# Router sums pinned later, further blocks spread over the expert loop, and each pair combined in two places

## The chip, the cores and the metric

One core of a Trainium2 chip runs the whole layer. The metric is the device time of one execution in microseconds.

## The reference

One decoder layer on 512 tokens of width 1024, in float32. A token mixer of three branches ends in an output projection; a layer norm follows; then a mixture of experts; then a second layer norm. What matters here, cut:

```python
x = layer_norm(DN_ALPHA * x + mix, ln1_g, ln1_b)
p_grp = softmax(x @ w_grp + b_grp)            # 4 groups, top 1
p_in  = softmax((x @ w_exp + b_exp)[group])   # 8 experts in the group, top 2
h = silu(xb @ w_gate[e]) * (xb @ w_up[e]);  y = h @ w_down[e]
x = layer_norm(DN_ALPHA * x + sum(weight * y), ln2_g, ln2_b)
```

32 experts of 512 hidden columns, gate, up and down of 2 MB each: 201 MB of weights that are read once.

## The kernel before

**Stages.** The token mixer runs until about 515 us. Then comes `out_proj` with the first norm and the router, then `moe`, the loop over 32 experts, then `final`, the second norm.

**The order.** A scheduler orders each engine's instructions by a model of their times. `keep_in_program_order` pins one instruction behind the one traced just before it on its engine. `inorder` does so when `self.steady` is set, which holds from the last token tile of `out_proj` through `moe`; so TensorE's order in the expert loop is the order of the program, and the other engines' order is the scheduler's.

**`out_proj`.** Two halves of 512 output columns, with products of split numbers (`mm3`, three matmuls each): the first half is 96 matmuls into four banks (4 blocks of `k` by 2 by 4 token tiles by 3), the second goes tile by tile, with transposes, `norm1` and the routing of each tile between. `router_consts` is called ahead of the first half. It loads router weights, biases and, as 4-element runs, the first norm's gain and bias `gb` by ScalarE's queue, multiplies them on VectorE (L933, L934), reduces them to `wsum` (L936), sums these over partitions with a matmul against ones (L938), and makes `nsg` and `br` of the result (L940, L941), which `norm1` uses (L1068, L1069).

**Weights.** SyncE's queue alone loads weights, in 192 pieces of 1 MB (`load_piece`, L1439), in the order in which the experts use them, into a ring of 20 slabs; up to eight are under way. A piece waits until its slab's last reader is done, and everything behind it on the queue waits too. One slab, the `G` slab (`spare`), also holds the gathered rows of pair 1 and, in its second half, small routing tables and then the gain and bias that `residual` uses; it joins the ring late, as the 39th piece.

**The expert loop.** Experts go in pairs of 128 gathered rows, 64 each. For expert `e` TensorE does 32 gate matmuls, the turn (transposes) of the hidden rows of expert `e-1`, 32 up matmuls, and after them `flush`, the `down` of expert `e-1`, whose result ScalarE and VectorE split into `yh` and `yl`. In an odd expert the rows of the next pair are transposed before the flush (`gather_turn`, two "s" banks, copied out by ScalarE and VectorE), and then `combine` adds the pair before to the four token tiles: 16 matmuls of one-hot rows `ot` against `y`, in banks "pt" and "s" by turns, and eight additions to `acc` on VectorE. PSUM has three "mm" banks, two "s", two "pt" and one "o".

**Only in the first experts.** `route_further` (after expert 1's flush, VectorE) finds the tokens beyond 64 of an expert; `slots_everywhere` (expert 2, before its flush) spreads the slots with 16 matmuls and two ScalarE copies; `further_slots` makes the tables of the further blocks with 24 small VectorE operations and eight small matmuls that add up in one "pt" bank, four before expert 2's flush and four after it. `residual` (experts 1 and 2, half of the columns each) loads gain and bias by ScalarE's queue, scales them there (L1089) and multiplies and adds them to `acc` on VectorE (L1092, L1093).

**The middle.** Before expert 16, `overflow` runs a loop over the further blocks, with a count read at run time. In these data the count is 0, so the loop is skipped, but every engine has to arrive (L1558) before any goes on. Sixteen pieces beyond that point are issued ahead of it.

Of the kernel before, what the change touches and what calls it, by code (L numbers as in the profile page):

```python
# [43 lines left out]
class Build:  # L44
# [869 lines left out]
    def router_consts(self, p):  # L914

        nc, I = self.nc, self.I
        V = nc.vector.tensor_tensor
        wr = p.tile([128, KD, 36], F32, name="wr")
        for i in range(2):
            ks = slice(i * 4, i * 4 + 4)  # L920
            nc.scalar.dma_start(wr[:, ks, 0:4], dram(I["router_w_grp"], i * 2048, [[16, 128], [4, 4], [1, 4]]))
            nc.scalar.dma_start(wr[:, ks, 4:36], dram(I["router_w_exp"], i * 16384, [[128, 128], [32, 4], [1, 32]]))
        br = p.tile([128, 36], F32, name="br")
        nc.scalar.dma_start(br[:, 0:4], dram(I["router_b_grp"], 0, [[0, 128], [1, 4]]))
        nc.scalar.dma_start(br[:, 4:36], dram(I["router_b_exp"], 0, [[0, 128], [1, 32]]))
        for i, nm in enumerate(("ln1_g", "ln1_b")):
            nc.scalar.dma_start(self.gb[:, i].rearrange("p (i k) -> p i k", i=2), dram(I[nm], 0, [[4, 128], [512, 2], [1, 4]]))
        ones = p.tile([128, KD, 128], F32, name="xT", bufs=2)[:, 0]
        nc.gpsimd.memset(ones, 1.0)
        bc = [128, KD, 36]  # L930
        wb = p.tile([128, KD, 128], F32, name="xT", bufs=2)[:, :, 0:36]
        sm = p.tile([128, 2, 36], F32, name="wsum")
        V(wb, wr, self.gb[:, 1, :, None].to_broadcast(bc), OP.mult)  # L933
        V(wr, wr, self.gb[:, 0, :, None].to_broadcast(bc), OP.mult)  # L934
        for i, t in enumerate((wr, wb)):
            nc.vector.tensor_reduce(sm[:, i], t.rearrange("p k n -> p n k"), axis=AX.X, op=OP.add)  # L936
        ps = self.bank("o")
        nc.tensor.matmul(ps[:, 0:72], ones, sm.rearrange("p i n -> p (i n)"), start=True, stop=True)  # L938
        nsg = p.tile([128, 36], F32, name="nsg")
        nc.vector.tensor_scalar(nsg, ps[:, 0:36], -1.0, None, op0=OP.mult)  # L940
        V(br, br, ps[:, 36:72], OP.add)  # L941
        return wr, nsg, br

    def out_proj(self, mh, ml):

# [4 lines left out]
        for tt in range(NT):  # L950
# [5 lines left out]
        rc = self.router_consts(p)  # L956

        def evac(half, tt, a):
            o = R[tt][:, half * 512:(half + 1) * 512]
# [12 lines left out]
                 for k4 in range(4)]  # L972
        for tt in range(NT):
            evac(0, tt, accs[tt])

        rows = [self.bank("s") for _ in range(2)]
        lg = p.tile([128, NT, 36], F32, name="lg")
# [94 lines left out]
    def norm1_apply(self, p, tt, mv, rs):  # L1072
# [7 lines left out]
            nc.scalar.activation(r[:, c], r[:, c], AF.Identity, bias=nm, scale=rs)  # L1080
        nc.gpsimd.dma_start(self.zd[tt * 128:(tt + 1) * 128], r)

    def residual(self, t, c):

        nc = self.nc
        cs = slice(c * 512, (c + 1) * 512)
        for i, nm in enumerate(("ln1_g", "ln1_b")):
            nc.scalar.dma_start(t[:, i], dram(self.I[nm], c * 512, [[0, 128], [1, 512]]))
        nc.scalar.mul(t, t, ALPHA)  # L1089
        for tt in range(NT):  # L1090
            r = self.acc[tt // 2][:, tt % 2, cs]
            self.tc.keep_in_program_order(nc.vector.tensor_tensor(r, r, t[:, 0], OP.mult))  # L1092
            nc.vector.tensor_tensor(r, r, t[:, 1], OP.add)  # L1093


    def first_max(self, p, v, rev, m, oh, name):
# [212 lines left out]
    def further_slots(self, part):  # L1309

        nc = self.nc
        T = nc.vector.tensor_scalar
        p = self.rt
        if part == 0:
            self.fps = self.bank("pt")[0:64, 0:32]
        for tt in (part * 2, part * 2 + 1):
            for i in range(2):
                rk = self.og0[:, tt % 2 * 2 + i, 0:64]
                wo = p.tile([128, 2, 16], F32, name="rwo", bufs=4)
                io, bk = self.io128[:, 0:16], self.blk[:, tt, i:i + 1]  # L1320
# [3 lines left out]
                self.inorder(nc.tensor.matmul(self.fps, rk, wo.rearrange("p a n -> p (a n)"), start=(tt == 0 and i == 0),  # L1324
                                              stop=(tt == NT - 1 and i == 1)))
        if part:
            T(self.idxo, self.fps[:, 0:16], 4096.0, None, op0=OP.add)
            for h in range(2):
                T(self.wt48[h * 64:(h + 1) * 64, 32:48], self.fps[:, 16:32], 0.5, None, op0=OP.mult)


    def gather(self, xs, idx):
# [75 lines left out]
            self.inorder(self.nc.tensor.matmul(ps, l, yh[:n, ds_], start=start and i == 0, stop=False))  # L1408
            self.inorder(self.nc.tensor.matmul(ps, l, yl[:n, ds_], start=False, stop=(i == len(terms) - 1)))  # L1409

    def combine(self):

        for tt in range(NT):
            for dh in range(2):
                ps = self.bank("s" if tt % 2 else "pt")
                self.combine_tile(ps, self.terms, tt, dh, True)
                a = self.acc[tt // 2][:, tt % 2, dh * 512:(dh + 1) * 512]
                self.nc.vector.tensor_tensor(a, a, ps, OP.add)  # L1418
        self.terms = []

    def ytile(self, last=False):
        t = self.moe_tile().bitcast(F32R) if last else self.slab("Y", "y", F32R)
# [29 lines left out]
    def moe(self):  # L1452
        p = self.ep
        self.worder, self.wt = [], []
        for e in range(E + 1):
            gu = [(e, m, i) for m in (0, 1) for i in (0, 1)] if e < E else []
            dn = [(e - 1, 2, i) for i in (0, 1)] if e else []
            self.worder += dn + gu if e == 2 * LOOP else gu + dn
        spare = self.spare
        xs1, gb = spare[:, :D], spare[:, D:].rearrange("p (i n) -> p i n", i=2)  # L1460
        xq = self.xq0
        xs = self.xq0.rearrange("p k n -> p (k n)")
        self.db = p.tile([128, 2, S], I16, name="db")
        pairs = E // 2
        pend = None
        self.terms = []

        def fetch(j, xs=xs):
            if j < pairs:
                self.gather(xs, self.idx[:, j:j + 1])  # L1470

        for e in range(E):
            pr, odd = e // 2, e % 2
            if pr == LOOP and not odd:
                self.flush(pend, self.turn(pend[1]))
                self.combine()
                pend = None

                held = self.worder.index((e, 0, 0)) + len(self.ring) - 7
                self.load_until(held)  # L1480
                self.overflow()
                self.npiece = held
                xq = self.gather_turn(xs)
                fetch(pr + 1)
            hT = []
            gu = self.gate_up(xq[:, :, odd * 64:(odd + 1) * 64], self.pieces(e, 0), self.pieces(e, 1),
                              (lambda: hT.append(self.turn(pend[1]))) if pend and e > 1 else None)
            if e == 0:
                self.load_until(len(self.first))
                fetch(1, xs1)  # L1490
                self.slot_weights()
                pend = (0, self.hidden(gu, self.wt48[:, 0:1]), None)
                continue
            if e == 1:
                fetch(2)
                hT.append(self.turn(pend[1]))
            if e == 2:
                self.slots_everywhere()
                self.further_slots(0)
# [260 lines left out]
```

## Time and profile before

| | us |
|---|---|
| median of three executions | 1097.99 |
| their range | 1094.75 to 1098.54 |
| the profiled execution | 1097.79 |
| its span | 1096.1 |
| TensorE, VectorE, ScalarE, GpSimd busy | 999.9, 593.6, 317.0, 201.1 |

The span is the stretch that the profile shows; 1.7 us of the time lie around it. Times in the rows are microseconds from the span's start. PE is TensorE's matmuls, PEld its weight loads, DVE VectorE, ACT ScalarE, POOL GpSimd, SP SyncE; a `q` behind the name is the engine's queue issuing something. A matmul's busy time overlaps the next one's, so TensorE's pace is read from the distance of starts.

### The profile page before, as it was taken

What the parts mean: (1) busy time and instruction counts of PE and PEld (TensorE: products, weight loads), DVE (VectorE), ACT (ScalarE), POOL (GpSimd) and SP (SyncE); (2) the same over time, 40 slices, a digit from 0 to 9 for tenths busy, and PEclk for the clock granted to TensorE, in tenths of its full rate; (3) what the DMA queues carried; (4) which work ended last, traced back from release to release, by engine and by line L of the source; (5) the groups of instructions that cost most, each with busy time, mean ns of one, the idle gap of its engine ahead of it and who ended that gap; (6) DMA issues with size and microseconds to landing.
All of it is one profiled execution on the core that took longest, in us unless ns stands there. A gap on an engine that the chain in (4) does not pass through costs nothing. (4 is left out here: it accounts for less than half of the span.)

```text
span 1096.1 us, 15867 instructions
## 1 busy us (share of the span) xinstructions
PE 999.9 (91%) x6189; PEld 698.7 (64%) x6189; DVE 593.6 (54%) x1427; ACT 317.0 (29%) x662; POOL 201.1 (18%) x179
## 2 busy tenths in 40 slices
PE   7969988999989999999698879999996999999994
PEld 6956676778778777888585455555552655555552
DVE  7992667474788784253255384444444244444436
ACT  4322222334556564232122121111110111111112
POOL 5410213334111223453112000000000000000003
PEclk9995999999999899999899989999998899999997
DMA  6701442225111112735415999999998999999992
GB/s 201 225 1 23 98 82 77 78 71 165 38 39 40 39 39 66 281 115 198 158 74 215 409 382 418 418 418 419 418 419 360 403 418 418 418 418 418 419 375 77
DMA packets 79821, 256.21 MB, mean 234 GB/s; under 512 B 16544, under 2 KB 43712, under 8 KB 55168
## 3 DMA queue, kind: packets, MB, share of 16 engines
q1 hardware_dynamic: 68064, 245.56, 57.4%
q10 hardware_dynamic: 8944, 3.59, 2.1%
q0 software_dynamic: 2736, 6.03, 1.5%
q8 instruction: 49, 0.80, 0.3%
q14 instruction: 28, 0.23, 0.1%
HBM read 254.40 MB, written 4.69 MB: 236 GB/s over the span
## 5 line engine op out<-in xcount | busy, mean ns | idle before, releaser
L1355 PE MATMUL ps_mm<-w,xq 128*64 128x256 f32 x1296 | 148.3, 381 | 0.0
L102 POOL TENSOR_TENSOR whl<-w,whl 128x1024 fp32r<-128x1024 f32 (+3 forms) x41 | 94.7, 2318 | 278.7 <-ACT whl L113 237.9
L1355 PEld LDWEIGHTS ps_mm<-w,xq 128*64 128x64 f32 x1296 | 91.2, 137 | 53.3 <-issue 8.6
L72 PE MATMUL ps_mm<-xh,whl 128*128 128x512 f32 x288 | 115.8, 402 | 0.0
L71 PE MATMUL ps_mm<-xl,whl 128*128 128x512 f32 x288 | 115.4, 401 | 0.0
L70 PE MATMUL ps_mm<-xh,whl 128*128 128x512 f32 x288 | 115.2, 400 | 0.0
L1365 DVE SCALAR_TENSOR_TENSOR th<-th,ps_mm 128x256 f32<-128x256 f32 x32 | 13.5, 421 | 161.2 <-ACT th L1364 161.2
L1393 DVE TENSOR_TENSOR y<-ps_o,y 64x512 fp32r<-64x512 f32 x60 | 41.3, 689 | 86.7 <-ACT y L1391 79.3
L1335 POOL DMA_INDIRECT xq<-zd,idx x14 | 14.0, 1003 | 389.8 <-PE ps_pt L1408 306.3
L1391 ACT CAST y<-ps_o 64x512 fp32r<-64x512 f32 x60 | 34.8, 579 | 141.7 <-issue 81.9
L1387 PE MATMUL ps_o<-w,hT 128*64 128x512 f32 x288 | 69.6, 608 | 0.0
L72 PEld LDWEIGHTS ps_mm<-xh,whl 128*128 128x128 f32 x288 | 54.7, 190 | 11.0 <-issue 0.8
L71 PEld LDWEIGHTS ps_mm<-xl,whl 128*128 128x128 f32 x288 | 54.8, 190 | 10.3
L70 PEld LDWEIGHTS ps_mm<-xh,whl 128*128 128x128 f32 x288 | 54.6, 189 | 10.4 <-issue 0.9
L113 ACT CAST whl<-w 128x1024 fp32r<-128x1024 f32 (+3 forms) x56 | 54.7, 989 | 13.5 <-PE ps_mm L72 13.4
L1355 PE MATMUL ps_mm<-rc,xq 128*64 128x256 f32 x384 | 46.8, 393 | 0.0
L1387 PEld LDWEIGHTS ps_o<-w,hT 128*64 128x64 f32 x288 | 21.4, 139 | 36.0 <-issue 33.0
L1364 ACT ACTIVATE th<-ps_mm 128x256 f32<-128x256 f32 x32 | 12.3, 383 | 104.8 <-PE ps_mm L1355 104.8
L1355 PE MATMUL ps_mm<-rd,xq 128*64 128x256 f32 x368 | 42.2, 381 | 0.0
L1355 PEld LDWEIGHTS ps_mm<-rc,xq 128*64 128x64 f32 x384 | 27.9, 142 | 17.6 <-issue 4.9
L1418 DVE TENSOR_TENSOR acc<-acc,ps_pt 128x512 f32<-128x512 f32 x60 | 38.4, 677 | 0.0
L1418 DVE TENSOR_TENSOR acc<-acc,ps_s 128x512 f32<-128x512 f32 x60 | 38.2, 677 | 0.0
(581 smaller groups left out, 2064.4 us busy)
## 6 DMA issues: line engine op xcount, KB each, us to landing
w<-in_moe_w_up_dram SPq DMA_DIRECT2D x43, 1024.0 KB, 19.9
w<-in_moe_w_gate_dram SPq DMA_DIRECT2D x38, 1024.0 KB, 20.3
w<-in_moe_w_down_dram SPq DMA_DIRECT2D x37, 1024.0 KB, 20.0
w<-in_w_in_dram SPq DMA_DIRECT2D x17, 1024.0 KB, 5.0
rc<-in_moe_w_down_dram SPq DMA_DIRECT2D x14, 1024.0 KB, 19.9
rc<-in_moe_w_gate_dram SPq DMA_DIRECT2D x14, 1024.0 KB, 19.9
rd<-in_moe_w_down_dram SPq DMA_DIRECT2D x13, 1024.0 KB, 20.5
rd<-in_moe_w_gate_dram SPq DMA_DIRECT2D x12, 1024.0 KB, 14.6
```

Of the source, the lines that this page charges most:

```text
L70: mm(ps, a[0], b[0], start=start, stop=False)
L71: mm(ps, a[0], b[1], start=False, stop=False)
L72: mm(ps, a[1], b[0], start=False, stop=stop)
L102: (V if eng == "dve" else P)(dst, src, h, OP.subtract)
L113: pin(self.nc.scalar.copy(hv[:, :, c:c + w], src))
L1335: self.nc.gpsimd.indirect_dma_start(xs[:n], None, self.zd[:, :], bass.IndirectOffsetOnAxis(ap=idx, axis=0), bounds_check=S - 1, oob_is_err ...
L1355: self.inorder(nc.tensor.matmul(gu[hh * 64:(hh + 1) * 64, part * 256:(part + 1) * 256], xe[:, k], w[k // 4][:, k % 4, hh * 256:(hh + 1) * ...
L1365: nc.vector.scalar_tensor_tensor(th, th, 1.0, gu[:, 0:256], op0=OP.add, op1=OP.mult)
L1387: self.inorder(nc.tensor.matmul(y[dh][dh * 64:(dh + 1) * 64], hT[:, q, hh * 64:(hh + 1) * 64], wd[f // 2][:, f % 2, dh * 512:(dh + 1) * 51 ...
L1391: nc.scalar.copy(part(yh, dh), y[dh][dh * 64:(dh + 1) * 64])
L1393: nc.vector.tensor_sub(part(yl, dh), y[dh][dh * 64:(dh + 1) * 64], part(yh, dh).bitcast(F32))
L1418: self.nc.vector.tensor_tensor(a, a, ps, OP.add)
```

## The change

Four parts.

- The sums' matmul with `nsg` and `br` becomes a function that `out_proj` calls after the first half's evacuation; the matmul is pinned there. The loads and products ahead of it stay.
- `residual` loses its loads and its scaling: `gains` issues the loads by GpSimd's queue, the first half at expert 0, the second at expert 1 after the first residual, and the factor goes into VectorE's operations. At expert 1 the residual now stands ahead of `route_further`.
- `slots_everywhere` and the first `slot_rows` move behind expert 2's flush; the two calls of `further_slots` move to experts 4 and 6, each summing in a bank of its own, with a small tile `rfs` between them.
- `combine` takes token tiles and bank tags: tiles 0 and 1 between gate and up of the odd expert, on "s" and "mm", tiles 2 and 3 where all four stood, on "pt" and "mm".

```diff
@@ router_consts, out_proj @@
-        ps = self.bank("o")
-        nc.tensor.matmul(ps[:, 0:72], ones, sm.rearrange("p i n -> p (i n)"), start=True, stop=True)
+        def sums():
+            ps = self.bank("o")
+            self.tc.keep_in_program_order(nc.tensor.matmul(ps[:, 0:72], ones, sm.rearrange("p i n -> p (i n)"), start=True, stop=True))
+            nc.vector.tensor_scalar(nsg, ps[:, 0:36], -1.0, None, op0=OP.mult)
+            V(br, br, ps[:, 36:72], OP.add)
...
             evac(0, tt, accs[tt])
+        sums()
@@ residual @@
+    def gains(self, t, c):
+        for i, nm in enumerate(("ln1_g", "ln1_b")):
+            nc.gpsimd.dma_start(t[:, i], dram(self.I[nm], c * 512, [[0, 128], [1, 512]]))
...
-            nc.scalar.dma_start(t[:, i], dram(self.I[nm], c * 512, [[0, 128], [1, 512]]))
-        nc.scalar.mul(t, t, ALPHA)
...
-            self.tc.keep_in_program_order(nc.vector.tensor_tensor(r, r, t[:, 0], OP.mult))
-            nc.vector.tensor_tensor(r, r, t[:, 1], OP.add)
+            self.tc.keep_in_program_order(nc.vector.scalar_tensor_tensor(r, r, ALPHA, t[:, 0], op0=OP.mult, op1=OP.mult))
+            nc.vector.scalar_tensor_tensor(r, t[:, 1], ALPHA, r, op0=OP.mult, op1=OP.add)
@@ further_slots @@
-            self.fps = self.bank("pt")[0:64, 0:32]
+            self.fsum = p.tile([64, 32], F32, name="rfs")
+        fps = self.bank("pt")[0:64, 0:32]
...
+            nc.vector.tensor_tensor(self.fsum, self.fsum, fps, OP.add)
...
+        else:
+            nc.vector.tensor_copy(self.fsum, fps)
@@ combine @@
-    def combine(self):
-        for tt in range(NT):
+    def combine(self, tiles=range(NT), tags=("pt", "s")):
+        for tt in tiles:
...
-                ps = self.bank("s" if tt % 2 else "pt")
+                ps = self.bank(tags[tt % 2])
@@ moe @@
+            def between():
+                hT.append(self.turn(pend[1]))
+                if self.terms:
+                    self.combine((0, 1), ("s", "mm"))
...
+                self.gains(gb, 0)
...
-            if e == 2:
-                self.slots_everywhere()
-                self.further_slots(0)
-                pend = (*pend[:2], self.slot_rows(self.sid[:, 0:1]))
+            if e in (4, 6):
+                self.further_slots(e // 2 - 2)
...
-                    self.combine()
+                    self.combine((2, 3), ("pt", "mm"))
...
-            if e == 1:
-                srt = self.route_further()
             if e == 2:
-                self.further_slots(1)
-                srt.close()
+                self.slots_everywhere()
+                self.terms[0] = (self.slot_rows(self.sid[:, 0:1]), *self.terms[0][1:])
             if e in (1, 2):
                 self.residual(gb, e - 1)
+            if e == 1:
+                self.gains(gb, 1)
+                srt = self.route_further()
```

## Rows read from the trace of the kernel before

**Rows 1.** The page: busy tenths of the DMA engines in 40 equal slices.
```profile
DMA  6701442225111112735415999999998999999992
```

**Rows 2.** Windows: stretch, length, busy of PE PEld DVE ACT POOL, PEclk, DMA, GB/s.
```profile
690.10:717.90 27.80, 27.14 (x190) 15.67 (x188) 11.67 (x22) 5.33 (x12) 1.00 (x1) 1.00 1.02 420
```

**Rows 3.** Chain of waits that ended last: start, length, what; the last expert.
```profile
1054.51 3.60 PE ps_mm L1355 x32
...
1063.30 3.58 PE ps_o L1387 x16
...
1070.74 0.57 PE ps_o L1387
```

**Rows 4.** Timeline of SyncE's queue; then DMA issues at 1044 to 1049, with landing.
```profile
1045.96 0.33 SPq L1439 DMA_DIRECT2D w<-in_moe_w_down_dram  x1
...
w<-in_moe_w_down_dram SPq DMA_DIRECT2D x1, 1024.0 KB, 20.0
```

**Rows 5.** Timeline, `out_proj`, first half: start, length, engine, line, operation, [idle before <-releaser].
```profile
515.10 0.39 PE L70 MATMUL ps_mm<-whl,mh 128*128 128x512 f32 x1
...
524.62 0.39 PE L70 MATMUL ps_s<-whl,mh 128*128 128x512 f32 x1
...
531.14 0.46 DVE L933 TENSOR_TENSOR xT<-wr,gb 128x288 f32<-128x288 f32 x1 [7.85 <-DMA rc<-in_moe_w_down_dram]
...
533.56 0.63 DVE L936 TENSOR_REDUCE wsum<-wr 128x36 f32<-128x288 f32 x1
...
534.34 0.67 PE L938 MATMUL ps_o<-wsum,xT 128*128 128x72 f32 x2 [9.34 <-DVE wsum L936]
...
538.19 0.40 PE L70 MATMUL ps_mm<-whl,mh 128*128 128x512 f32 x1
...
548.20 0.39 PE L72 MATMUL ps_s<-whl,ml 128*128 128x512 f32 x1
```

**Rows 6.** Windows of two stretches, and SyncE's queue as expert 0 begins.
```profile
534.80:538.20 3.40, 3.40 (x10) 2.68 (x11) 0.29 (x2) 0.93 (x1) 0.00 (x0) 0.53 0.58 243
...
590.00:597.50 7.50, 5.69 (x54) 3.81 (x56) 3.66 (x16) 2.46 (x9) 1.11 (x1) 1.00 0.01 3
...
597.55 0.33 SPq L1439 DMA_DIRECT2D w<-in_moe_w_up_dram  x1
```

**Rows 7.** Waits at 560 to 662: who <- for whom: total, times, longest.
```profile
ACT w L1089 <- DMA w<-in_ln_b_dram: 26.0, 2, 13.4
...
SPq L1439 <- PE ps_o L1387: 11.5, 1, 11.5
```

**Rows 8.** Windows: expert 2's stop, and the notch in the loads after it.
```profile
631.00:639.30 8.30, 1.77 (x13) 1.23 (x12) 8.27 (x28) 0.96 (x2) 0.00 (x0) 0.86 1.01 419
...
640.00:655.00 15.00, 15.00 (x102) 10.23 (x98) 10.60 (x29) 3.52 (x7) 0.31 (x1) 0.87 0.95 352
```

**Rows 9.** Groups by line, 470 to 700: busy, mean ns of one, idle before.
```profile
L1092 DVE TENSOR_TENSOR acc<-acc,w 128x512 f32<-128x512 f32 x8 | 5.5, 682 | 0.5 <-ACT w L1089 0.5
...
L960 DVE SCALAR_TENSOR_TENSOR acc<-acc,ps_mm 128x512 f32<-128x512 f32 x6 | 4.1, 684 | 15.4 <-PE ps_mm L72 15.4
```

**Rows 10.** Timeline of one pair's combination, and of `y` and the turn after it.
```profile
711.91 0.19 PEld L1408 LDWEIGHTS ps_s<-y,ot 128*128 128x128 f32 x1 [1.09 <-ACT xq L1246]
...
714.91 0.20 PEld L1387 LDWEIGHTS ps_o<-w,hT 128*64 128x64 f32 x4 [0.37 <-issue]
...
803.35 1.39 DVE L1393 TENSOR_TENSOR y<-ps_o,y 64x512 fp32r<-64x512 f32 x2 [2.19 <-ACT y L1391]
...
805.43 0.32 PEld L1374 LDWEIGHTS ps_pt<-ident,th 128*128 128x128 f32 x2 [0.39 <-issue]
```

**Rows 11.** SyncE's queue about the skipped loop, and the window of its end.
```profile
828.47 0.33 SPq L1439 DMA_DIRECT2D rc<-in_moe_w_up_dram  x1
849.00 0.34 SPq L1439 DMA_DIRECT2D w<-in_moe_w_up_dram  x1
...
843.00:850.00 7.00, 0.54 (x3) 0.54 (x4) 1.81 (x5) 0.00 (x0) 0.00 (x0) 0.66 0.41 159
```

More of the change, by code (lines that the diff above doesn't have):

```diff
@@ L936, in router_consts @@
             nc.vector.tensor_reduce(sm[:, i], t.rearrange("p k n -> p n k"), axis=AX.X, op=OP.add)
-        ps = self.bank("o")
-        nc.tensor.matmul(ps[:, 0:72], ones, sm.rearrange("p i n -> p (i n)"), start=True, stop=True)
         nsg = p.tile([128, 36], F32, name="nsg")
-        nc.vector.tensor_scalar(nsg, ps[:, 0:36], -1.0, None, op0=OP.mult)
-        V(br, br, ps[:, 36:72], OP.add)
-        return wr, nsg, br
+        def sums():
[3 more added lines that the diff above has]
+            V(br, br, ps[:, 36:72], OP.add)
+        return (wr, nsg, br), sums
     def out_proj(self, mh, ml):
@@ L955, in out_proj @@
               for j in range(2)] for i in range(2)]
-        rc = self.router_consts(p)
+        rc, sums = self.router_consts(p)
         def evac(half, tt, a):
@@ L1081, in norm1_apply @@
         nc.gpsimd.dma_start(self.zd[tt * 128:(tt + 1) * 128], r)
+    def gains(self, t, c):
+        nc = self.nc
+        for i, nm in enumerate(("ln1_g", "ln1_b")):
+            nc.gpsimd.dma_start(t[:, i], dram(self.I[nm], c * 512, [[0, 128], [1, 512]]))
     def residual(self, t, c):
@@ L1086, in residual @@
         cs = slice(c * 512, (c + 1) * 512)
-        for i, nm in enumerate(("ln1_g", "ln1_b")):
-            nc.scalar.dma_start(t[:, i], dram(self.I[nm], c * 512, [[0, 128], [1, 512]]))
-        nc.scalar.mul(t, t, ALPHA)
         for tt in range(NT):
             r = self.acc[tt // 2][:, tt % 2, cs]
-            self.tc.keep_in_program_order(nc.vector.tensor_tensor(r, r, t[:, 0], OP.mult))
-            nc.vector.tensor_tensor(r, r, t[:, 1], OP.add)
+            self.tc.keep_in_program_order(nc.vector.scalar_tensor_tensor(r, r, ALPHA, t[:, 0], op0=OP.mult, op1=OP.mult))
+            nc.vector.scalar_tensor_tensor(r, t[:, 1], ALPHA, r, op0=OP.mult, op1=OP.add)
     def first_max(self, p, v, rev, m, oh, name):
@@ L1323, in further_slots @@
                 T(wo[:, 1], io, bk, self.wk[:, i, tt:tt + 1], op0=OP.is_equal, op1=OP.mult)
-                self.inorder(nc.tensor.matmul(self.fps, rk, wo.rearrange("p a n -> p (a n)"), start=(tt == 0 and i == 0),
-                                              stop=(tt == NT - 1 and i == 1)))
+                self.inorder(nc.tensor.matmul(fps, rk, wo.rearrange("p a n -> p (a n)"), start=(tt % 2 == 0 and i == 0),
+                                              stop=(tt % 2 == 1 and i == 1)))
         if part:
-            T(self.idxo, self.fps[:, 0:16], 4096.0, None, op0=OP.add)
+            nc.vector.tensor_tensor(self.fsum, self.fsum, fps, OP.add)
+            T(self.idxo, self.fsum[:, 0:16], 4096.0, None, op0=OP.add)
             for h in range(2):
-                T(self.wt48[h * 64:(h + 1) * 64, 32:48], self.fps[:, 16:32], 0.5, None, op0=OP.mult)
+                T(self.wt48[h * 64:(h + 1) * 64, 32:48], self.fsum[:, 16:32], 0.5, None, op0=OP.mult)
+        else:
+            nc.vector.tensor_copy(self.fsum, fps)
     def gather(self, xs, idx):
@@ L1418, in combine @@
                 self.nc.vector.tensor_tensor(a, a, ps, OP.add)
-        self.terms = []
+        if NT - 1 in tiles:
+            self.terms = []
     def ytile(self, last=False):
@@ L1485, in moe @@
             hT = []
+            def between():
+                hT.append(self.turn(pend[1]))
+                if self.terms:
+                    self.combine((0, 1), ("s", "mm"))
             gu = self.gate_up(xq[:, :, odd * 64:(odd + 1) * 64], self.pieces(e, 0), self.pieces(e, 1),
-                              (lambda: hT.append(self.turn(pend[1]))) if pend and e > 1 else None)
+                              between if pend and e > 1 else None)
             if e == 0:
@@ L1496, in moe @@
                 hT.append(self.turn(pend[1]))
-            if e == 2:
-                self.slots_everywhere()
-                self.further_slots(0)
-                pend = (*pend[:2], self.slot_rows(self.sid[:, 0:1]))
+            if e in (4, 6):
+                self.further_slots(e // 2 - 2)
+                if e == 6:
+                    srt.close()
             end = pr == pairs - 1
```

## The prediction, made before the changed kernel was seen

> **What bounds the kernel now.** I read the page's slices first, to see where the DMA engines are full, then the windows over the expert loop, then the chain of waits at the end, and only then the timelines of the two places where the loads are not full.
>
> From about 600 us to 1066 us the DMA engines are full but for two notches [rows 1]. One pair of experts takes 27.8 us there, TensorE never rests for long, and the DMA engines run at 420 GB/s, 1.02 of their time [rows 2]. So both are near their limit, and they have to be told apart. A pair needs 12 pieces of 1,048,576 bytes and a gather of 0.52 MB, 13.1 MB, which at 418 GB/s is 31.3 us (an estimate from these rows; one piece is 2.51 us). TensorE takes 27.8 us a pair and so eats 3.5 us a pair of the stock that was loaded ahead. At the end the stock is nearly gone: the last weight piece is issued at 1045.96 us, takes 20.0 us to land, 1065.96 us, and the last `down` begins at 1070.74 us [rows 3, 4]. The loop is thus held by TensorE, with the loads 4.8 us behind it. If TensorE alone gets faster, those 4.8 us are all there is. For more, the stream of loads must start earlier or lose its notches.
>
> **The router's sums.** In the first half of `out_proj` TensorE starts a matmul each 0.227 us (42 steps from 515.10 to 524.62 us). Then it stands until 534.34 us, because the sums' matmul (L938) sits in the middle of the half and waits for `wsum`. VectorE can't make `wsum` before the small loads of gain and bias land: it waits 7.85 us for them and ends `wsum` at 534.2 us. After that TensorE runs near the 1.2 GHz level (granted 0.53) until 538.19 us [rows 5, 6]. The row names a weight load as what VectorE waited for, but L933 reads only `wr` and `gb`, and those are the loads issued last on ScalarE's queue. 96 matmuls at 0.227 us would put the last start at 515.10 + 95 x 0.227 = 536.6 us; it is 548.2 us. Lost: 11.6 us.
>
> After the change the matmul is pinned behind the last matmul of that half, at about 536.9 us. `wsum` is there since 534.2 us, 2.7 us earlier, so nothing waits. The sums still cost their two matmuls, 0.67 us at the lower clock, about 0.35 us at the higher. Their followers on VectorE (`nsg`, `br`) are two small operations, needed only by the first `norm1` some 20 matmuls later. Gain: 11.6 - 0.4 = **11.2 us**. What is late next in this half is nothing that I find: the parts of the second half need buffers that TensorE frees as it goes, and these come free earlier by the same amount.
>
> From 548 us to expert 0 the work is a chain of compute. The first load that opens the full stream is issued at 597.55 us, when expert 0 has freed a slab; before it, from 590 to 597.5 us, the DMA engines do nothing (0.01) [rows 6]. So TensorE and the stream both start 11.2 us earlier.
>
> **Gains by another queue, further blocks later.** Before, ScalarE issues the loads of gain and bias and then waits for them at the head of its queue, 26.0 us in two waits [rows 7]. Behind it stand the copies that feed `down`. Expert 2 also holds `further_slots`, for which TensorE waits on VectorE: of 8.3 us it works 1.77 [rows 8]. While TensorE stands, slabs don't come free: SyncE's queue waits 11.5 us for a `down` [rows 7], and the DMA engines fall to 352 GB/s over 15 us [rows 8]. That notch is 15 x (418 - 352) / 418 = **2.4 us** of loads.
>
> The change takes the wait from ScalarE. GpSimd issues the four loads; behind them on its queue stand only the gathers, needed half a pair later. VectorE's sixteen operations stay sixteen: a scalar_tensor_tensor of this shape is 684 ns, the multiply 682 ns [rows 9], so folding in the factor costs nothing. The route's operations on VectorE now come behind the first residual (8 x 0.68 = 5.5 us), so `slots_everywhere` may wait for `dd` up to 5.5 us. The second residual may wait for its load up to 13 us, the longest such wait before [rows 7], with VectorE's later work behind it. Both lie on TensorE's side only. The 24 small operations of `further_slots`, two additions on `fsum` and its eight matmuls move to experts 4 and 6, beside matmuls. I take the notch as gone: 2.4 us, bounds 0 and 2.4.
>
> **The combination in two places.** In each odd expert the second group of combining matmuls waits 1.09 us for a bank that the gather's copies still read [rows 10]. The new first half stands between gate and up on one "s" pair and one "mm" pair, where no copy is running; the second half uses "pt" and "mm". Matmuls and additions are as many as before. The new risk is `y`: the additions need the pair's second `down`, whose subtraction ends at 803.35 + 1.39 = 804.7 us, while the half would begin after the turn at 805.43 us plus 0.4 us. That leaves about 1 us, so no wait. Value: about 1.1 us a pair for TensorE, bounds 0 and 1.5, and **nothing** on the clock while the loads hold the pair at 31.3 us.
>
> **The middle.** At the skipped loop of further blocks SyncE issues nothing from 828.5 to 849.0 us, since every engine has to arrive; the eight loads under way run dry, and 843 to 850 us moves 159 GB/s [rows 11], 7 x 259 / 418 = **4.3 us** of loads. TensorE arrives later than the loads by a stock that the change makes smaller: TensorE gains 11.2 us, the stops of expert 1 and 2 and 5 x 1.1 us until there, the loads 13.6 us. By some 13 us it comes earlier against them, and the notch is 4.3 us. I take all of it; bounds 0 and 4.3.
>
> **The sum.** The last piece lands at 1065.96 - 11.2 - 2.4 - 4.3 = 1048.1 us. TensorE has gained at least 11.2 + 6.5 (expert 2's stop) + 13 x 1.1 = 32 us, so it now waits for loads. The last `up` lands four pieces earlier, 1038.1 us; then its 16 matmuls (half of 3.60), half a combination (2.0, as 12 of its matmuls take 3.0), `down` of expert 30 (3.58), the opening matmuls of two tiles and a turn (3.9, from that `down`'s end to the next) and the last `down` (3.6) [rows 3, 10]: 1053.0 us, where it now ends at 1074.3. That is 21.3 us. The profiled execution took 1097.79 us with a span of 1096.1, 0.2 below the median of 1097.99. 1097.8 - 21.3 = **1076.5 us**.
>
> **The rivals.** First, **only the start moves**: the notches stay, because the second residual's load or the barrier stops SyncE's queue as before, or the sums' loads land more than 2.7 us later than here and part of the stop stays (the change then doesn't do what it says in that place). With 11.2 us alone it is 1087 us. For it: both new loads of gain and bias go through full DMA engines. Against it: up to eight loads of 2.51 us are under way, so a stop of the queue must outlast 20 us. Second, **the stream opens earlier still**: SyncE's queue keeps its order, and at 597.55 us one slab's wait holds back four pieces for other memory. If these pass it, up to 8 us of idle DMA time [rows 6] are used: 1068 us. Third, **slower by the clock**: once TensorE waits for each piece, about 0.8 us in 2.5, the granted clock falls to 1.2 GHz, and a pair costs some 53 us in place of 31.3. One such pair eats the gain; with two it is about 1120 us. For it: after the stop at 524.8 us TensorE ran at the lower level for 3.9 us [rows 5, 6]. Against it: from 590 to 597.5 us TensorE worked 5.69 of 7.5 us in short stretches and the granted clock stayed 1.00 [rows 6], and at the lower level TensorE becomes the slower side, works without a stop and gets its clock back.
>
> The Trainium skill speaks for this third case: "TensorE: Matmul & The Clock Gate", section "HAM oscillation — how this bites in real kernels", tells of a loop that waits for a DMA at each weight tile and falls to half clock at every one. By that rule the last pairs would be slower as priced above. The row from 590 to 597.5 us doesn't agree for waits as short as these; no row here has a longer run of them.
>
> **How the numbers follow.** Forecast 0.62, only the start 0.20, earlier stream 0.12, clock 0.06. The range reaches from the earlier stream to the start alone, 1067 to 1088 us; it takes in both notches kept (1083) and leaves out the clock. A measurement of this kernel can tell about 0.5 per cent, 5.5 us, from no change. Faster 0.91, same 0.04, slower 0.05.
>
> **What would show it.** No stop of TensorE before the sums, and the first half of `out_proj` some 22 us long; expert 0 about 11 us earlier; no ScalarE wait for gain and bias; 418 GB/s without notches until about 1048 us; TensorE's waits for weights in the last pairs at the clock 1.00. The forecast is wrong if the loads stop anywhere for over 5 us, or if TensorE still has no wait for weights at the end.

## The result, and the profile after

Four executions of the changed kernel have a median of 1083.57 us (1082.55 to 1084.53), four of the kernel before on the same chip 1097.71 us. The ratio is 0.988, with a 95 per cent interval of 0.985 to 0.990. The forecast was 1076.5 us, so of 21.3 us forecast some 14 came. The profiled execution took 1082.7 us and has a span of 1081.0 us, 15.1 less than the one before; the profiles are compared with each other below.

First the stretch ahead of the experts. The timeline of the changed kernel, first TensorE in the first half of `out_proj`, then VectorE:

```profile
514.59 0.39 PE L70 MATMUL ps_mm<-whl,mh 128*128 128x512 f32 x1
...
536.12 0.39 PE L72 MATMUL ps_s<-whl,ml 128*128 128x512 f32 x1
536.35 0.34 PE L941 MATMUL ps_o<-wsum,xT 128*128 128x72 f32 x2
...
530.41 0.46 DVE L933 TENSOR_TENSOR xT<-wr,gb 128x288 f32<-128x288 f32 x1 [7.75 <-DMA gb<-in_ln_b_dram]
...
532.88 0.67 DVE L936 TENSOR_REDUCE wsum<-wr 128x36 f32<-128x288 f32 x1
```

VectorE still waits 7.75 us for gain and bias, and now the row names that load. But `wsum` is done at 533.55 us, 2.8 us before the sums' matmul wants it, so TensorE no longer stops. The half takes 21.5 us (514.59 to 536.12) where it took 33.1 [rows 5].

Then SyncE's queue in the changed kernel, at the start of the stream, about the skipped loop, and at the last weight pieces:

```profile
585.66 0.33 SPq L1450 DMA_DIRECT2D w<-in_moe_w_up_dram  x1
...
813.67 0.33 SPq L1450 DMA_DIRECT2D rc<-in_moe_w_up_dram  x1
834.50 0.34 SPq L1450 DMA_DIRECT2D w<-in_moe_w_up_dram  x1
...
1021.56 0.33 SPq L1450 DMA_DIRECT2D rc<-in_moe_w_up_dram  x1
...
1026.56 5.30 SPq L1450 DMA_DIRECT2D w<-in_moe_w_down_dram  x3
```

The stream opens 11.9 us earlier than in [rows 6]. The stop at the skipped loop is as long as in [rows 11]: 20.8 us where it was 20.5. The third of the last three weight pieces goes out at 1026.56 + 5.30 - 0.33 = 1031.53 us, 14.4 us earlier than in [rows 4].

Windows of the changed kernel (columns as in [rows 2]): the time ahead of the stream, the place of the old notch, the stop at the loop, and a stretch near the end.

```profile
580.00:585.00 5.00, 4.32 (x47) 2.89 (x47) 2.45 (x8) 2.08 (x6) 0.49 (x1) 1.00 0.02 3
...
640.00:655.00 15.00, 15.00 (x118) 10.49 (x114) 7.11 (x21) 1.91 (x4) 0.00 (x0) 1.00 1.01 418
...
830.00:835.00 5.00, 0.22 (x1) 0.23 (x2) 0.30 (x1) 0.00 (x0) 0.00 (x0) 0.50 0.33 138
835.00:840.00 5.00, 5.00 (x34) 3.53 (x35) 2.27 (x6) 1.50 (x4) 1.00 (x1) 0.72 0.85 324
...
1000.00:1005.00 5.00, 3.98 (x24) 1.36 (x22) 0.36 (x1) 1.16 (x2) 0.00 (x0) 1.00 1.01 421
```

The notch of 352 GB/s [rows 8] is gone; the one at the loop is not. In the last window TensorE waits for loads (3.98 us busy of 5), at a granted clock of 1.00. The first such wait behind the loop is this one, in the timeline of the changed kernel:

```profile
1001.44 1.94 PE L1397 MATMUL ps_o<-w,hT 128*64 128x512 f32 x8 [0.45 <-DMA w<-in_moe_w_down_dram]
```

Until then TensorE works from the stock that was loaded while it stood at the loop. Seven waits for loads, of 0.45 to 0.63 us, come in the last two pairs.

The chain of waits that ended last, in the changed kernel (start, length, what), about the loop and at the end:

```profile
813.67 20.41 DMA rc<-in_moe_w_up_dram
834.08 0.70 issue
834.78 1.98 PE ps_s L1352 x8
...
985.26 21.13 DMA rd<-in_moe_w_gate_dram
...
1016.43 20.04 DMA w<-in_moe_w_gate_dram
1036.51 1.95 PE ps_mm L1365 x16
...
1042.64 1.05 PE ps_s L1553 x2
1043.70 1.88 PE ps_mm L1365 x16
...
1050.56 1.87 PE ps_o L1397 x8
...
1055.43 0.57 PE ps_o L1397
```

Before, the last expert's part of this chain was TensorE's [rows 3]; now it goes mostly from load to load until 1036.51 us (TensorE holds 10 us of it, from 1006.44 to 1016.40 us) and is TensorE's from there. Its first row is the key to the miss: what the loop waited for is the landing of the last piece that SyncE had issued. VectorE and TensorE had been done for some 19 and 20 us (timeline of the changed kernel):

```profile
814.15 1.28 DVE L1428 TENSOR_TENSOR acc<-acc,ps_s 128x512 f32<-128x512 f32 x2
...
834.78 1.98 PE L1352 MATMUL ps_s<-ident,xq 128*128 128x128 f32 x8 [20.90 <-DMA rc<-in_moe_w_up_dram]
```

To compare kernels whose earlier stages differ by a microsecond or so, three marks are read in each (us): S, the issue of the first piece that opens the full stream; W, the issue of the last weight piece; and the span's end. Each ratio is against the kernel before on the same chip. The kernel before has a median of 1097.71 us beside the changed kernel, of 1095.70 us beside the four runs below it, of 1094.64 us beside fewer_ahead, tail, open and open_tail and of 1095.27 us beside no_last_combine and open_three; so across rows compare the ratios, and not the medians to a microsecond or two. S, W and the stop are from one profiled execution each. S alone differs by 2.6 us (583.93 to 586.57) between kernels that are the same up to there.

| kernel | S | stop at the loop | S to W | W to the end | median, us | ratio to before (95 per cent) |
|---|---|---|---|---|---|---|
| before | 597.55 | 20.5 | 448.4 | 50.1 | 1097.71 | |
| changed | 585.66 | 20.8 | 445.9 | 49.5 | 1083.57 | 0.988 (0.985 to 0.990) |
| sums_only | 584.78 | 21.0 | 448.7 | 49.9 | 1085.62 | 0.991 (0.988 to 0.994) |
| early_experts_back | 586.57 | 21.6 | 450.8 | 49.3 | 1084.80 | 0.989 (0.987 to 0.991) |
| one_place | 586.29 | 20.7 | 445.8 | 50.1 | 1082.17 | 0.987 (0.984 to 0.989) |
| no_loop | 585.37 | none | 442.7 | 48.9 | 1078.51 | 0.984 (0.981 to 0.986) |
| fewer_ahead | 584.20 | 22.1 | 447.3 | 49.5 | 1082.99 | 0.989 (0.987 to 0.992) |
| no_last_combine | 585.58 | 21.1 | 446.2 | 49.1 | 1082.22 | 0.987 (0.985 to 0.989) |
| tail | 583.93 | 20.3 | 446.5 | 54.6 | 1086.74 | 0.992 (0.990 to 0.995) |

The changed kernel's 15.1 us of span are thus 11.9 at S, 2.5 between S and W, and 0.7 behind W.

### The profile page after: what moved, and what is told of

Its sections match the earlier page's. It is cut to its first block, busy times and chain, and to the rows that moved or that the text cites. A ratio compares the mean times of both kernels' runs of the same rounds, so it can differ in the third digit from the quotient of the medians.

```text
span 1081.0 us, 15903 instructions
## 1 busy us (share of the span) xinstructions
PE 990.0 (92%) x6189; PEld 693.8 (64%) x6189; DVE 595.4 (55%) x1429; ACT 315.1 (29%) x660; POOL 203.8 (19%) x183
## 5 line engine op out<-in xcount | busy, mean ns | idle before, releaser
L70 PEld LDWEIGHTS ps_mm<-xh,whl 128*128 128x128 f32 x288 | 54.6, 190 | 10.5 <-issue 0.9
L1385 ACT COPY hT<-ps_pt 128x256 f32<-128x256 f32 x32 | 11.9, 372 | 94.4 <-PE ps_pt L1384 94.4
L858 ACT ACTIVATE P<-P,mx 128x128 f32<-128x128 f32 (+3 forms) x64 | 35.9, 563 | 6.8 <-DVE mx L856 6.7
## 6 DMA issues: line engine op xcount, KB each, us to landing
w<-in_moe_w_up_dram SPq DMA_DIRECT2D x43, 1024.0 KB, 20.4
w<-in_moe_w_down_dram SPq DMA_DIRECT2D x37, 1024.0 KB, 20.5
rd<-in_moe_w_gate_dram SPq DMA_DIRECT2D x12, 1024.0 KB, 20.5
```

Source lines behind the costliest of these rows:

```text
L70: mm(ps, a[0], b[0], start=start, stop=False)
L858: nc.scalar.activation(t, t, AF.Exp, scale=-1.0, bias=mx[:, hh, br:br + 1], accum_out=sm[:, hh, br:br + 1])
```

## The experiments

**The sums alone** (sums_only): the kernel before with this edit.

```diff
-        ps = self.bank("o")
-        nc.tensor.matmul(ps[:, 0:72], ones, ...)
+        def sums():
+            ps = self.bank("o")
+            self.tc.keep_in_program_order(nc.tensor.matmul(ps[:, 0:72], ones, ...))
...
+        sums()
```

> The kernel before with the move of the router's sums alone. Theory (the start is worth its full length, and nothing takes it back): the first load that opens the full stream is issued about 11.5 us earlier than in the kernel before (597.55 us), the notch at 640 to 655 us only moves and stays, SyncE still stops some 20.5 us at the skipped loop, the last weight piece is issued about 11.5 us earlier than 1045.96 us, and the time is about 1086.5 us. Rival (the earlier start is partly taken back later, because TensorE and the loads meet in other places): the last piece gains less than 9 us and the time is 1089 us or more.

1085.62 us. S comes 12.8 us earlier, S to W is that of before within 0.3 us, and W to the end too. The start was worth its full length and nothing gave it back. Most of what the whole change gains is here: 12.7 of 15.1 us in the spans, and by the ratios some 9.5 of 13.6 us.

**The early experts put back** (early_experts_back): the changed kernel without the second and third part of the change; its edits, cut:

```diff
-                self.gains(gb, 0)
...
-            if e in (4, 6):
-                self.further_slots(e // 2 - 2)
...
+            if e == 2:
+                self.slots_everywhere()
+                self.further_slots(0)
```

> The changed kernel with the gains, the residual, the spreading of the slots and the further blocks put back to ScalarE's queue and to expert 2; the sums and the two places of the combination stay. Theory (the notch at 640 to 655 us is what this part was worth, 2.4 to 2.9 us of loads): the stop of TensorE in expert 2 and a window at about 350 GB/s come back, the last weight piece is issued 2.5 to 3 us later than in the changed kernel (1031.53 us), and the time is 1086 to 1086.5 us. Rival (TensorE's stop matters for itself, some 6.5 us): 1089 us or more. Second rival (the stock that the loads have there covers it): 1083.5 us, no change.

1084.80 us; its four executions lie between 1084.28 and 1088.31, so the time alone can't tell it from the changed kernel. The profile can, though it is that of the slowest of the four (1088.31 us, the others at most 1085.07). Windows of early_experts_back:

```profile
615.00:630.00 15.00, 8.58 (x70) 5.96 (x68) 14.39 (x53) 1.93 (x4) 0.00 (x0) 0.84 1.02 421
630.00:645.00 15.00, 15.00 (x91) 9.91 (x90) 11.02 (x30) 2.59 (x4) 0.00 (x0) 0.82 0.83 304
```

TensorE's stop is back (8.58 us busy of 15), and behind it the notch, now 304 GB/s. S to W is 4.9 us longer than in the changed kernel, 1.9 us more than the theory's upper end; about 0.8 of it is a longer stop at the loop. That this part fills the notch is shown. Its price is less sure: 2.8 us by the profile of sums_only, 4.9 us by this slowest execution, and some 1.5 us by the ratios.

**The combination in one place again** (one_place), from the changed kernel:

```diff
                 hT.append(self.turn(pend[1]))
-                if self.terms:
-                    self.combine((0, 1), ("s", "mm"))
...
-                    self.combine((2, 3), ("pt", "mm"))
+                    self.combine()
```

> The changed kernel with all four token tiles combined in one place again, in banks pt and s by turns. Theory (the loads hold the pairs at 31.3 us, so TensorE's 1.1 us a pair are worth nothing but once, in the last pair, where TensorE's own chain ends last): the wait of about 1.1 us for a bank comes back in each pair, the last weight piece is issued within 0.5 us of 1031.53 us, and the time is 1083.5 to 1085 us. Rival (the two places were worth their 1.1 us in each of 14 pairs, or in all pairs up to the skipped loop): 1088 us or more.

1082.17 us, the same as the changed kernel. The wait is back in each pair; TensorE's weight loads in the timeline of one_place:

```profile
714.12 0.19 PEld L1418 LDWEIGHTS ps_s<-y,ot 128*128 128x128 f32 x1 [1.09 <-ACT xq L1252]
```

S to W doesn't move (445.8 and 445.9 us). W to the end is 0.6 us longer, so the 1.1 us count at most once, in the last pair.

**Without the skipped loop** (no_loop): the changed kernel without the line below, that is without the loop over further blocks, whose body never runs in these data.

```diff
-                self.overflow()
```

> The changed kernel without the loop over further blocks (the loop and its tables for it are left out; the count is 0 in these data, so the loop's body never ran). Theory (the loop's entry waits until every load under way has landed, which drains the DMA engines, whatever TensorE's lead is; the forecast's 4.3 us are there, but the change could not take them): the stop of SyncE's queue of 20.8 us and the two windows at 138 and 324 GB/s go, the last weight piece is issued 4 to 5 us earlier than 1031.53 us, and the time is 1078.5 to 1080 us. Rival (TensorE's 20 us of standing still are the price, not the loads): 1070 us or less. Second rival (the loads that the stop holds back are made up later): 1083 us, no change.

1078.51 us. Timeline of SyncE's queue in no_loop:

```profile
813.35 0.33 SPq L1450 DMA_DIRECT2D rc<-in_moe_w_up_dram  x1
815.94 0.33 SPq L1450 DMA_DIRECT2D w<-in_moe_w_up_dram  x1
...
1023.06 5.31 SPq L1450 DMA_DIRECT2D w<-in_moe_w_down_dram  x3
```

and a window of no_loop:

```profile
870.00:900.00 30.00, 27.43 (x186) 14.87 (x184) 11.76 (x22) 5.33 (x12) 1.00 (x1) 1.00 1.01 419
```

The queue goes on without a stop. S to W falls by 3.2 us, W to the end by 0.6, the median by 5.1 (4.4 by the ratios). So the loop's price is some 4 us, 3.2 of them in the loads. The 20.9 us that TensorE stands there in the changed kernel (813.88 to 834.78 us) are not it: without the loop TensorE waits for the loads in small pieces instead, 27.43 us busy of 30.

**Fewer pieces ahead of the loop** (fewer_ahead). This run tells what ends the stop.

```diff
-                held = self.worder.index((e, 0, 0)) + len(self.ring) - 7
+                held = self.worder.index((e, 0, 0)) + len(self.ring) - 15
```

> The changed kernel with eight pieces fewer issued ahead of the skipped loop (five beyond that point in place of thirteen). Theory (the loop is left when the last load under way has landed and the last engine has come): the last piece ahead is issued about 794 us and lands about 814 us, VectorE comes at 815.4 us as before, so SyncE goes on at 816 to 818 us in place of 834.5 us, and TensorE stands for 3 us in place of 21; the loads are dry 2 to 3 us longer than in the changed kernel, and the time is 1083 to 1087 us. Rival (the loop is left a fixed 19 us after VectorE has come, as the changed kernel alone would also have it): SyncE goes on at 834.5 us, the loads are dry for 20 us and the time is 1100 us or more. Second rival (left 6.3 us after the last engine, as the kernel before would also have it): 821.7 us, and 1088 to 1090 us.

1082.99 us. (Ahead of the loop thirteen pieces are issued, five in this run; the sixteen in the description of the kernel was a miscount.) Timeline of fewer_ahead, SyncE's queue and VectorE's last work ahead of the loop:

```profile
792.35 22.40 SPq L1450 DMA_DIRECT2D w<-in_moe_w_gate_dram  x2
814.80 1.29 SPq L1450 DMA_DIRECT2D w<-in_moe_w_up_dram  x2
...
812.77 1.28 DVE L1428 TENSOR_TENSOR acc<-acc,ps_s 128x512 f32<-128x512 f32 x2
```

The first row holds two issues, the last one ahead of the loop at 792.35 us and the first one behind it at 792.35 + 22.40 - 0.33 = 814.42 us. VectorE ends at 814.05 us. The last piece, issued at 792.35 us, took 20.4 us to land and was there at 812.8 us. So here the loads have landed first, and the loop is left 0.4 us after the last engine; neither rival (834.5 or 821.7 us) is near. In the changed kernel VectorE has ended at 815.4 us, and the loop is left when the piece of 813.67 us has landed, at 834.1. The later of the two decides, and the loop itself costs 0.4 us. TensorE's stand shrinks to about 2 us and the time stays the same, which again says that its stand has no price here. S to W is 1.5 us longer, since the loads lie dry a little longer.

**Work moved ahead of the last pair's loads** (tail). Pair 14's last `down` and its whole combination come earlier:

```diff
-            self.worder += dn + gu if e == 2 * LOOP else gu + dn
+            self.worder += dn + gu if e in (2 * LOOP, E - 2) else gu + dn
...
+            if e == E - 2:
+                self.flush(pend, self.turn(pend[1]))
+                pend = None
```

> The changed kernel with the two down pieces of expert 29 loaded ahead of expert 30's gate, its down run ahead of that gate, and the combination of pair 14 done within expert 30. Theory (in the changed kernel the end is set by TensorE's own 22.5 us behind the landing of expert 31's second gate piece, not by the last piece; work that is moved ahead of that landing fills waits for loads): the last weight piece is issued at the same time (1031.5 us, give or take 0.5), the last down ends about 54 us after expert 31's second gate piece was issued becomes some 38 to 39, that is 4 us or more earlier (1054 to 1055 us in place of 1059.0), and the time is 1078.5 to 1080 us. Rival (TensorE has no waits ahead of that piece that could hold 7 us more of work, so the work only moves): 1082 to 1084 us.

1086.74 us, with a ratio above the changed kernel's though their intervals touch (0.990); the seven executions spread from 1083.62 to 1090.22, three of them at the rival's upper end. So the gain forecast is refuted, and some loss is likely. In the profiled execution, the median one, W to the end grows by 5.1 us. Timeline of tail, VectorE and TensorE:

```profile
1020.85 1.39 DVE L1403 TENSOR_TENSOR y<-ps_o,y 64x512 fp32r<-64x512 f32 x2 [1.78 <-ACT y L1401]
1022.34 5.16 PE L1397 MATMUL ps_o<-w,hT 128*64 128x512 f32 x16 [2.35 <-issue]
...
1058.08 0.61 PE L1397 MATMUL ps_o<-w,hT 128*64 128x512 f32 x1 [2.74 <-issue]
```

and a window of tail:

```profile
1022.30:1024.50 2.20, 2.16 (x6) 0.86 (x8) 0.00 (x0) 0.00 (x0) 0.00 (x0) 0.50 1.02 425
```

Two waits lie open here that the changed kernel hides in its last pair. The moved `down` comes right behind another one, with only a turn between, and starts after 2.35 us without work, 0.1 us after VectorE has finished the split of that one (1020.85 + 1.39 = 1022.24 us). It starts at the lower clock (0.50) and takes 5.16 us in place of 3.6. And the last `down` waits 2.74 us while ScalarE and VectorE split the `down` before it; in the changed kernel the openings of the final tiles fill that gap. From 1005 us on TensorE waits for no load any more, so it had little to fill with the moved work. The theory that moving work ahead of the landing brings the end forward falls.

**The last combination left out** (no_last_combine): the changed kernel without pair 14's sums, 16 matmuls and eight additions.

```diff
-                if self.terms:
+                if self.terms and e < E - 1:
                     self.combine((0, 1), ("s", "mm"))
...
+                if end:
+                    self.terms = []
```

> The changed kernel without the combination of pair 14 in expert 31 (the sums of that pair are left out, 16 matmuls and eight additions). Theory (behind the landing of expert 31's second gate piece TensorE has some 22.5 us of its own work, more than the loads behind it need, so what is taken out there comes off the end): the last weight piece is issued as before (1031.5 us, give or take 1), the last down ends 3 to 4 us earlier against that issue (27.5 us behind it in the changed kernel), and the time is 1079.5 to 1081 us. Rival (the last piece, which lands 20 us after its issue, holds the last down): no change against that issue, 1083 to 1084 us.

1082.22 us, and W to the end is 49.1 us in place of 49.5: 4 us of TensorE's work gave 0.4. Timeline of TensorE in no_last_combine:

```profile
1052.21 0.95 PE L1397 MATMUL ps_o<-w,hT 128*64 128x512 f32 x1 [2.74 <-DVE rd L1403]
```

and a window of no_last_combine:

```profile
1052.20:1055.70 3.50, 3.49 (x8) 0.81 (x8) 0.00 (x0) 0.00 (x0) 0.00 (x0) 0.52 0.11 43
```

The last `down` starts 3.2 us earlier (1052.21 against 1055.43 us), as the theory had it: the work taken out does move its start. But it waits for the same split, runs its first half at the lower clock and has an opening of 1.1 us between its halves, which in the changed kernel comes behind it; so it ends at 1058.7 us where it ended at 1059.0. The last piece does not hold it, but only just: it is due at 1051.7 us (1031.80 + 19.9), 0.5 us before the start. So neither the theory's gain nor the rival's cause came out.

**The stream opened earlier.** In the changed kernel the DMA engines move 3 GB/s from 580 to 585 us, because the ring's first piece, which waits for expert 0's slab, stands ahead of four pieces for other memory (`rd`). Run open pins it behind them (the first part of the diff), open_three has the second part too and takes only three of them ahead, and open_tail joins open and tail.

```diff
+        if len(self.wt) == len(self.first):
+            self.tc.add_manual_dep(d.ins, self.prior.ins.name, ...)
...
-        self.first += [(rd, "rd", ND)] * ND
+        self.first += [(rd, "rd", ND)] * (ND - 1)
```

> The changed kernel with one load pinned on SyncE's queue: the piece that waits for expert 0's first slab comes behind the four pieces for other memory in place of ahead of them. Theory (that memory is free when the last matmul of the output projection is done, about 573 us, and the DMA engines do next to nothing from 577 to 585 us): the four pieces are issued from 573 to 576 us in place of 586, all later pieces come 8 to 10 us earlier, TensorE starts expert 0 up to 4 us later because the gather of its rows shares the engines, the last weight piece is issued 7 to 9 us earlier than 1031.5 us, and the time is 1075 to 1077 us. Rival (the four pieces' memory comes free no earlier than that slab): 1083 us, no change. Second rival (the gather and the stores of the normed rows are held up by the loads, and expert 0 starts 8 us later): the later pieces wait for slabs again and the time is 1080 us or more.

> Both edits of the two runs before it, on the changed kernel. Theory (the loads hold the loop from start to end and both edits act on the loads' path, one at its start and one behind its end): the gains add, 12 to 14 us, and the time is 1070 to 1072 us. Rival (with the loads 8 us earlier TensorE becomes the slower side in the last pairs, and the second edit gives nothing): 1075 to 1077 us.

> The changed kernel with three pieces in place of four taken into the rd memory before the ring begins, and the ring's first piece pinned behind the third. Theory (in the run with four, three pieces went out at 571 us and the fourth waited until 586.7 us for memory that GpSimd's routing tables still use, which held back the ring's first piece by some 4 us): the three pieces go out as early as there, the ring's first piece goes out when expert 0 frees its slab (some 14 us after them), the last weight piece is issued 6 to 8 us earlier than in the changed kernel, measured from the issue of the two up pieces ahead of the stream (466.9 us from their first in the changed kernel), and the time is 1074 to 1077 us. Rival (one slab less in the first round lets TensorE and the loads wait for each other in the first experts): 1080 us or more.

open: 1079.63 us (1076.40 to 1080.75; the profile is that of the fastest), ratio 0.986 (0.983 to 0.988), less than expected. Timeline of open, SyncE's queue and GpSimd:

```profile
570.90 0.33 SPq L1450 DMA_DIRECT2D rd<-in_moe_w_down_dram  x1
571.28 0.90 SPq L1450 DMA_DIRECT2D rd<-in_moe_w_gate_dram  x2
586.68 0.33 SPq L1450 DMA_DIRECT2D rd<-in_moe_w_up_dram  x1
587.11 0.38 SPq L1450 DMA_DIRECT2D w<-in_moe_w_up_dram  x1
...
586.04 0.61 POOL L1039 TENSOR_TENSOR w<-O,wt 128x256 bf16<-128x256 bf16 x1 [0.29 <-DVE wt L1038]
```

Three pieces go out at 571 us. The fourth goes out just after GpSimd's routing tables end (586.65 us), and with it everything behind it waits. From the two `up` pieces ahead of the stream to W it is 463.6 us, where the changed kernel takes 466.9. open_tail took 1082.49 us (0.988, 0.986 to 0.991). From the `up` pieces to W it is 463.4 us, as in open, and W to the end is 53.4 us, so the second edit costs 3.9 us there and 5.1 alone. The difference is about what the lower clock cost in tail, for here the same wait leaves the clock at 1.00 (timeline and window of open_tail):

```profile
1018.84 3.65 PE L1397 MATMUL ps_o<-w,hT 128*64 128x512 f32 x16 [2.35 <-issue]
...
1018.80:1021.00 2.20, 2.16 (x10) 0.92 (x12) 0.00 (x0) 0.00 (x0) 0.00 (x0) 1.00 1.01 421
```

open_three leaves the fourth piece to the ring:

```profile
570.90 0.33 SPq L1450 DMA_DIRECT2D rd<-in_moe_w_down_dram  x1
571.28 0.90 SPq L1450 DMA_DIRECT2D rd<-in_moe_w_gate_dram  x2
582.57 2.06 SPq L1450 DMA_DIRECT2D w<-in_moe_w_up_dram  x2
...
1022.88 0.33 SPq L1450 DMA_DIRECT2D rd<-in_moe_w_down_dram  x1
```

It takes 1074.06 us (1072.69 to 1078.3), ratio 0.981 (0.979 to 0.983), and is the fastest kernel here. From the two `up` pieces to W it is 461.3 us, 5.6 less than in the changed kernel, a little under the theory's 6 to 8; W to the end is 49.4 us, as ever. What the loads gain at the start goes to the end in full.

## Why the prediction was right in part

**What bounds the kernel: right.** It was said that both sides are near their limit and that TensorE's own time would become worth nothing. The chain of the changed kernel is mostly loads from the loop to 1036.51 us, TensorE waits for loads from 1001 us on, one_place shows the bank waits of all pairs worth nothing, and each term that moved the loads moved the end.

**The sums: right.** Forecast 11.2 us, measured 11.6 us in that half (33.1 to 21.5) and 11.9 us at S, of which 0.5 us was there ahead of the half (514.59 against 515.10 us). The margin of `wsum` was 2.8 us, forecast 2.7. That S agrees to within a microsecond is in part luck, as S differs by 2.6 us between kernels alike up to there.

**The early notch: right, a little small.** Forecast 2.4 us of loads. From S to the last piece ahead of the loop it is 230.9 us before and 228.0 after: 2.9 us.

**The combination: right.** No bank wait and no wait for `y` in the pairs that are combined in two places, and nothing on the clock. (The combination ahead of the skipped loop keeps its one place and its two waits for `y`, 0.67 and 0.82 us, as before.)

**The middle: wrong, the first of two failed steps.** The step reads that the stop at the skipped loop lasts until "every engine has to arrive", that TensorE comes 13 us earlier against the loads, and that the 4.3 us notch therefore goes. The engines did come earlier, at 815.4 us, and the stop stayed 20.8 us, because it ends with the landing of SyncE's own last piece. [rows 11] and [rows 4] held the hint side by side: 849.00 - 828.47 = 20.5 us is the time that one piece takes to land with eight under way (20.0 us). The bound from below, nothing, was the right value. Where no_loop takes the stop away, the loads gain 3.2 us between S and W, so the size of 4.3 us was high too. The prediction's own sign, 418 GB/s without notches, failed here: 138 and 324 GB/s from 830 to 840 us.

**The end: wrong, the second failed step.** It was reckoned that the last `up` lands four pieces ahead of the last piece, that TensorE stands ready, and that 14.9 us of work follow; so the tail gains 3.4 us on top of the loads. Measured, W to the end shrinks by 0.7 us. What failed is that TensorE stands ready. The last `up` was issued at 1021.56 us and, at 19.9 us for its landing, was there at 1041.5, but TensorE came to its second half at 1043.70: behind the gate piece that landed at 1036.51 it has gate, turn, half a combination, the first half of `up` and an opening to do, 7.2 us, while the loads need 5.0 for the two `up` pieces. That is 2.2 us of the 2.7 us missing; the work behind it was near the forecast, 15.3 us (to 1059.0) against 14.9. And in no_loop, where TensorE waits for loads in every pair from 848 us on, W to the end is still 48.9 us. So before the change only some 1.3 us were to be had there, though the last `down` began 4.8 us behind the landing of its weights. That gap was the time of a chain (`up`, combination, `down`, split, `down`) and no slack for the loads. How short this chain could be is open: in the changed kernel the split of the `down` before the last ends at 1055.1 us, 0.3 us ahead of the last `down`, and both tries, tail and no_last_combine, ran into it.

**Together**: 0.5 + 11.4 (sums) + 2.9 (early notch) - 0.4 (the loop and behind it) + 0.7 (end) = 15.1 us against 11.2 + 2.4 + 4.3 + 3.4 = 21.3. Two of the four terms came out and two did not; that the time still lies in the range stated is owed to the range's width, for its upper end was the start alone.

**The rivals.** Only the start moves: false for the early notch, true for the middle. The stream opens earlier still: false for this change, since SyncE's queue kept its order; the idle time it spoke of was real, as open_three shows. Slower by the clock: false. TensorE waits for pieces in the last pairs at a granted clock of 1.00, and in no_loop it does so from 848 us on, at 1.00 as well.

The Trainium skill ("TensorE: Matmul & The Clock Gate", section "HAM oscillation — how this bites in real kernels") tells of a loop that falls to half clock at every wait for a load, with waits several times as long as the 0.45 to 0.63 us that come up in the last two pairs of the changed kernel. For these short waits the traces don't show it. Behind single longer waits, none of them for a load, they show both: 0.50 and 0.52 behind 2.35 us in tail and 2.74 us in no_last_combine, 1.00 behind 2.35 us in open_tail and 2.74 us in tail.

## What to carry to other kernels

A stop of a queue that is as long as one transfer takes to land is a wait for that landing: compare the two lengths before giving it to the engines that come late. Where the loads hold the loop, only what moves the loads counts: their start, and each place where their queue stands behind a wait that another piece does not have. A gap between a landing and its use is slack only if the engine has no chain of its own to that use; read the chain back from the use, not from the landing.

## What the runs showed of the hardware that was not expected

- SyncE leaves the entry of a skipped loop only when the last piece that it issued has landed, not only when the engines have come: 20.3 to 21.6 us from the last issue in ten kernels, and 22.1 us where the last engine came later than the landing. Behind the later of the two it is 0.4 us. Whether the chip asks for this or the program's own semaphores do, no run here tells.
- TensorE standing for 20.9 us in the middle of the kernel cost nothing measurable of its own (fewer_ahead cuts it to some 2 us, and its span is the same, 1081.0 us), since the loads ran on for most of it.
- The granted clock behind waits of the same length differs: 0.50 in tail and 1.00 in open_tail behind 2.35 us, 0.52 in no_last_combine and 1.00 in tail behind 2.74 us. What makes the difference is not settled.
